# Two operand tiles of TensorE moved up by 32 bytes in SBUF

## The chip, the core and the metric

The kernel runs on one core of one Trainium2 chip. The metric is the time that the device takes for one execution, in microseconds (us). TensorE (PE) does the matrix products, VectorE (DVE) and ScalarE (ACT) the elementwise work, GpSimd (POOL) issues some transfers and SyncE (SP) the others. SBUF is the on-chip memory: 128 partitions, in each of which a tile lies at one byte address. A product on TensorE has a stationary operand, brought in by a weight load (LDWEIGHTS, "PEld" in the profile), and a moving operand, which the MATMUL instruction streams past it. Both are read from SBUF.

## The reference, cut to what matters

One decoder layer on 256 tokens of width 2048, in float32:

```
proj = x @ W_in                                    # q, k, v of 16 heads
mix  = concat(diff_attention, moba_attention) @ W_out
h    = LayerNorm(2**0.25 * x + mix)
u    = h @ W_up                                    # a gate and a value half, 5632 columns each
ffn  = (silu(causal_conv3(u_gate)) * u_value) @ W_down
out  = LayerNorm(2**0.25 * h + ffn)
```

## The kernel before, in words

**Number format.** TensorE works on float32r operands. To keep the accuracy of float32, each operand is split into a high part (ACT copies it to float32r, line 128 or 797) and a low part (DVE subtracts the high part, line 129 or 807; some low parts are made by an accumulating transfer, line 805). Each product is then three: high times high, high times low, low times high, all added up in PSUM.

**Operand tiles.** The input's parts are the tiles `xa` and `xb` (line 145), the normed tokens' parts `ha` and `hb` (line 528); both come from the helper `two` (line 139), under the tags `t2a` and `t2b` of the pool `keep`, so that h takes over the place of x. Each holds, for 8 chunks of 128 features, 256 high and 256 low values side by side, 16,384 bytes in a partition. Later three other tiles use the same places: `z2` (line 1356, tag `t2a`), `rawt` (line 1290) and `gb2` (line 1424, both `t2b`). Weights come through 4 buffers `raw` (1 MB each) into 6 buffers `hl` (high and low parts of 128x1024). Everything that TensorE reads as float32r begins, in every buffer, at a byte address that leaves 128 when it is divided by 512, and all slices of it that an instruction takes begin a multiple of 512 bytes further on. So any two float32r operands are at the same address modulo 512 bytes.

**Three kinds of products.** They differ in what moves and what stands still.

- *Pairs* (lines 206 to 211 for q and k, 831 to 834 for the up projection): a 128x128 block of the weights is stationary and the tokens move. The high block meets high and low tokens side by side, 512 columns; then the low block meets the high tokens alone, 256 columns. A pair of such instructions is done 16 times for each 128 features of the output:

```
for k in range(8 * x, 8 * x + 8):
    o = slice(k % 8 * P, k % 8 * P + P)
    mm(dst, wh[:, o], at_k(h2, k).rearrange("p j t -> p (j t)"), k == 0, False)
    mm(dst[:, 0:S], wl[:, o], at_k(h2, k)[:, 0], False, k == KT - 1)
```

- *Products with x or h stationary*: v (line 452, the weights move, 512 columns) and the first tile of the up projection (`mm_first`, lines 567 to 569, 256 columns).
- *All others*: the output projection (`mm_o`, line 499), the down projection (lines 1070 to 1072 and 1134 to 1136) and the last tiles (1365 to 1367). Their stationary operands are `mh`, `ml`, `aparts`, `pparts` and `tails`, the weights move, 512 columns mostly. They touch neither x nor h.

All of them go through the helper `mm`, so the profile names them all by line 202 and tells them apart by their tiles.

**Order of the work.** First v, q and k of four heads at a time, with the attention of earlier heads in between; then the output projection; the first LayerNorm with `mm_first`; then the up projection. From a certain tile on, products of the down projection come between its tiles, by a list that a planner in the kernel orders (lines 651 to 756, with costs and due times written in it). At the end come the last products of the down projection and the second LayerNorm. The planner knows nothing of addresses.

Of the kernel before, what the change touches and what calls it, by code (L numbers as in the profile page):

```python
# [11 lines left out]
F32 = mybir.dt.float32  # L12
# [4 lines left out]
P = 128  # L17
# [33 lines left out]
def hymba_layer(ctx: ExitStack, tc: tile.TileContext, a: dict):  # L51
# [3 lines left out]
    def pool(name, bufs=1, space=None):  # L55
        kw = {} if space is None else {"space": space}
        return ctx.enter_context(tc.tile_pool(name=name, bufs=bufs, **kw))

    keep = pool("keep")
    raws = pool("raws", 4)  # L60
    splits = pool("splits", 6)
    small = pool("small")
# [76 lines left out]
    def two(name):  # L139
        return [keep.tile([P, KT // 2, 2, S], F32R, name=f"{name}{j}", tag=f"t2{j}") for j in "ab"]  # L140
# [2 lines left out]
        return t[k // 8][:, k % 8] if n is None else t[k // 8][:, k % 8:k % 8 + n]  # L143

    x2 = two("x")
    z = keep.tile([P, 2, D], F32, name="z", tag="z")
    xraw = z.rearrange("p t d -> p (t d)")

# [1420 lines left out]
```

## Time and profile before

| | before |
|---|---|
| median of 3 runs | 1126.47 us (1125.85 to 1126.74) |
| the profiled execution's own time | 1125.76 us |
| its span, first to last instruction | 1124.0 us |
| PE busy | 1108.2 us, 99% |
| PE weight loads busy | 941.5 us, 84% |
| DVE busy | 917.3 us, 82% |
| ACT busy | 702.8 us, 63% |
| granted TensorE clock, mean | 0.996 |

Busy times of matmuls overlap: an instruction of 512 columns is in flight for some 390 ns, and the next one begins long before it ends. So the mean duration of a group is not the time that one of them takes of the engine; that is the distance from one start to the next, to be had from the number of instructions in a stretch in which PE never waits.

### The profile page before, as it was taken

What the parts mean: (1) busy time and instruction counts of PE and PEld (TensorE: products, weight loads), DVE (VectorE), ACT (ScalarE), POOL (GpSimd) and SP (SyncE); (2) the same over time, 40 slices, a digit from 0 to 9 for tenths busy, and PEclk for the clock granted to TensorE, in tenths of its full rate; (3) what the DMA queues carried; (4) which work ended last, traced back from release to release, by engine and by line L of the source; (5) the groups of instructions that cost most, each with busy time, mean ns of one, the idle gap of its engine ahead of it and who ended that gap; (6) DMA issues with size and microseconds to landing.
All of it is one profiled execution on the core that took longest, in us unless ns stands there. A gap on an engine that the chain in (4) does not pass through costs nothing.

```text
span 1124.0 us, 15532 instructions
## 1 busy us (share of the span) xinstructions
PE 1108.2 (99%) x5878; PEld 941.5 (84%) x5878; DVE 917.3 (82%) x1485; ACT 702.8 (63%) x1022; POOL 75.8 (7%) x90
## 2 busy tenths in 40 slices
PE   9999999999999999999999999999999999999995
PEld 6888888888888898888888888888888888888884
DVE  6886886867745787789999777798999888898997
ACT  6565465444544396767777666767767676767671
POOL 0000000000000000000100100000100010001104
PEclk9999999999999999999999999999999999999998
DMA  8755454545455637777897878777887698769883
GB/s 329 292 225 197 151 169 168 182 156 188 150 187 192 220 128 264 246 260 239 263 248 248 231 229 268 222 245 222 223 253 226 224 247 262 219 218 268 246 262 127
DMA packets 48507, 249.89 MB, mean 222 GB/s; under 512 B 4784, under 2 KB 6704, under 8 KB 27824
## 3 DMA queue, kind: packets, MB, share of 16 engines
q1 hardware_dynamic: 39360, 221.11, 55.0%
q0 software_dynamic: 9072, 27.79, 13.7%
q8 instruction: 46, 0.75, 0.3%
q14 instruction: 29, 0.24, 0.1%
HBM read 216.90 MB, written 9.44 MB: 201 GB/s over the span
## 4 chain that ended last, share of the span: by engine, by line
PE 93%; DVE 4%; DMA 1%; ACT 1%; issue 0%; POOL 0%; SPq 0%; POOLq 0%; ACTq 0%; DVEq 0%
PE bank L202 92%; DVE st L391 1%; DMA raw<-in_w_d 1%; DVE z L388 1%; PE bank L325 0%; DMA raw<-in_w_v 0%; DVE z L1460 0%; DVE bparts L1021 0%; DVE hl L1325 0%; DVE z L1371 0%; DVE spill L1384 0%; PE bank L542 0%; ACT bparts L1017 0%; DVE z L1456 0%; PE bank L372 0%
## 5 line engine op out<-in xcount | busy, mean ns | idle before, releaser
L202 PE MATMUL bank<-hb,hl 128*128 128x512 f32 x1376 | 256.7, 339 | 0.0
L202 PE MATMUL bank<-ha,hl 128*128 128x512 f32 x1376 | 255.6, 338 | 0.0
L202 PEld LDWEIGHTS bank<-ha,hl 128*128 128x128 f32 x1376 | 214.4, 188 | 33.7 <-ACT ev L901 0.4
L202 PEld LDWEIGHTS bank<-hb,hl 128*128 128x128 f32 x1376 | 210.7, 188 | 31.9
L129 DVE TENSOR_TENSOR hl<-raw,hl 128x1024 fp32r<-128x1024 f32 (+1 forms) x143 | 164.7, 1163 | 68.9 <-ACT hl L128 68.5
L128 ACT ACTIVATE hl<-raw 128x1024 fp32r<-128x1024 f32 (+1 forms) x143 | 143.7, 1009 | 92.8 <-PE bank L202 65.0
L807 DVE TENSOR_TENSOR hl<-raw,hl 128x1024 fp32r<-128x1024 f32 x128 | 154.9, 1221 | 20.9 <-ACT hl L797 20.4
L797 ACT ACTIVATE hl<-raw 128x1024 fp32r<-128x1024 f32 x128 | 133.0, 1052 | 35.1 <-PE bank L202 32.7
L901 ACT ACTIVATE ev<-bank 128x512 f32<-128x512 f32 x86 | 51.3, 597 | 96.5 <-PE bank L202 96.4
L202 PE MATMUL bank<-bparts,aparts 128*128 128x512 f32 x432 | 109.9, 392 | 0.8 <-DVE bparts L1021 0.8
L1021 DVE TENSOR_TENSOR bparts<-sums,bparts 128x1024 fp32r<-128x1024 f32 x72 | 85.9, 1222 | 20.0 <-ACT bparts L1017 20.0
L202 PE MATMUL bank<-xa,hl 128*128 128x512 f32 (+1 forms) x512 | 97.7, 344 | 0.0
L202 PE MATMUL bank<-xb,hl 128*128 128x512 f32 (+1 forms) x512 | 96.3, 341 | 0.0
L202 PEld LDWEIGHTS bank<-bparts,aparts 128*128 128x128 f32 x432 | 78.4, 188 | 18.2 <-DVE bparts L1021 1.6
L202 PEld LDWEIGHTS bank<-xa,hl 128*128 128x128 f32 x512 | 78.9, 188 | 13.5 <-issue 1.3
L202 PEld LDWEIGHTS bank<-xb,hl 128*128 128x128 f32 x512 | 78.4, 189 | 11.7
L1017 ACT ACTIVATE bparts<-sums 128x1024 fp32r<-128x1024 f32 x72 | 73.2, 1054 | 17.4 <-PE bank L202 8.1
L805 POOL DMA_DIRECT2D hl<-raw x39 | 34.1, 875 | 548.2 <-ACT hl L795 377.7
L202 PE MATMUL bank<-hl,mh 128*128 128x512 f32 x256 | 70.4, 392 | 0.0
L202 PE MATMUL bank<-hl,aparts 128*128 128x512 f32 x252 | 65.4, 391 | 0.0
L795 ACT ACTIVATE hl<-raw 128x1024 fp32r<-128x1024 f32 x39 | 41.2, 1055 | 29.8 <-PE bank L202 29.7
L202 PEld LDWEIGHTS bank<-hl,mh 128*128 128x128 f32 x256 | 47.7, 188 | 9.7
(167 smaller groups left out, 1426.7 us busy)
## 6 DMA issues: line engine op xcount, KB each, us to landing
raw<-in_w_u SPq DMA_DIRECT2D x88, 1024.0 KB, 5.6
raw<-in_w_d SPq DMA_DIRECT2D x42, 1024.0 KB, 6.7
raw<-in_w_qk SPq DMA_DIRECT2D x32, 1024.0 KB, 4.8
hl<-raw POOLq DMA_DIRECT2D x41, 512.0 KB, 5.4
raw<-in_w_o SPq DMA_DIRECT2D x16, 1024.0 KB, 4.8
raw<-in_w_v SPq DMA_DIRECT2D x12, 1024.0 KB, 4.8
zd<-spill POOLq DMA_DIRECT2D x20, 256.0 KB, 7.5
raw<-in_w_v SPq DMA_DIRECT2D x8, 256.0 KB, 4.6
```

Source lines behind the costliest of these rows:

```text
L128: ACT.activation(hi[:, s], t[:, x:y], AF.Copy)
L129: DVE.tensor_tensor(lo[:, s], t[:, x:y], hi[:, s].bitcast(F32), ALU.subtract)
L202: PE.matmul(out, lhsT, rhs, start=start, stop=stop)
L388: DVE.scalar_tensor_tensor(z[:, t, s], z[:, t, s], alpha, src, op0=ALU.mult, op1=ALU.add)
L391: DVE.bn_stats(stats[ln, t][:, c], z[:, t, s])
L795: ACT.activation(lo, raw_of[n][:, s], AF.Copy, scale=-1.0)
L797: ACT.activation(hi, raw_of[n][:, s], AF.Copy)
L805: POOL.dma_start(lo, raw_of[n][:, s], accum_op=ALU.add)
L807: DVE.tensor_tensor(lo, raw_of[n][:, s], hi.bitcast(F32), ALU.subtract)
L901: ACT.activation(evs[n], bank[b], AF.Copy)
L1017: ACT.activation(U()["b", j][:, 0], U()["T"][:, 2 * j:2 * j + 2], AF.Copy)
L1021: DVE.tensor_tensor(b[:, 1], U()["T"][:, 2 * j:2 * j + 2], b[:, 0].bitcast(F32), ALU.subtract)
```

## The change

Two tiles are added to the pool `keep`. One of 32 bytes lies ahead of `xa` and `xb`, one of 480 bytes behind them. Nothing reads or writes them. By that, `xa`, `xb`, `ha`, `hb`, and the later tiles on their places (`z2`, `rawt`, `gb2`), begin at an address that leaves 160 when it is divided by 512, 32 bytes more than before. All tiles behind them lie 512 bytes higher, so their address modulo 512 is the same as before, 128 for all other float32r operands.

```diff
@@ -57,6 +57,7 @@
     keep = pool("keep")
+    shift = keep.tile([P, 8], F32, name="shift")
     raws = pool("raws", 4)
     splits = pool("splits", 6)
@@ -143,6 +144,7 @@
     x2 = two("x")
+    back = keep.tile([P, P - 8], F32, name="back")
     z = keep.tile([P, 2, D], F32, name="z", tag="z")
```

The instructions, their order on each engine, their waits and the transfers are the same, one by one; only addresses differ.

## The prediction

> **What bounds the kernel now.** I read the page first: the share of each engine, the clock row and the summary of the chain that ended last.
>
> ```profile
> span 1124.0 us, 15532 instructions
> PE 1108.2 (99%) x5878; PEld 941.5 (84%) x5878; DVE 917.3 (82%) x1485; ACT 702.8 (63%) x1022; POOL 75.8 (7%) x90
> PEclk9999999999999999999999999999999999999998
> PE 93%; DVE 4%; DMA 1%; ACT 1%; issue 0%; POOL 0%; SPq 0%; POOLq 0%; ACTq 0%; DVEq 0%
> ```
>
> TensorE is never short of work, its clock is granted in full, and 93% of the last chain is its own matmuls. So the time is set by how far apart the matmuls start. The only thing that this change can touch is that distance, and it touches it only if it depends on where the operands lie. Next I looked in the chain of waits, told in order of time, for long pieces of PE without a wait; the columns are start, length, engine and count.
>
> ```profile
> 413.37 69.35 PE bank L202 x400
> 485.60 578.32 PE bank L202 x3061
> ```
>
> The first piece is the up projection alone: 400 matmuls are 200 pairs (one of 512 columns, one of 256), so a pair takes 69.35 / 200 = 346.8 ns. The second piece is the up projection with products of the down projection between its tiles. Its content is in the groups by line and shape for 486 to 1063 us, with a count, the busy time and the mean ns of one instruction:
>
> ```profile
> L202 PE MATMUL bank<-hb,hl 128*128 128x512 f32 x584 | 210.0, 399 | 0.0
> L202 PE MATMUL bank<-ha,hl 128*128 128x512 f32 x584 | 208.7, 397 | 0.0
> L202 PE MATMUL bank<-hb,hl 128*128 128x256 f32 x584 | 164.0, 281 | 0.0
> L202 PE MATMUL bank<-ha,hl 128*128 128x256 f32 x584 | 163.8, 281 | 0.0
> L202 PE MATMUL bank<-bparts,aparts 128*128 128x512 f32 x416 | 105.6, 391 | 0.6 <-DVE bparts L1021 0.6
> L202 PE MATMUL bank<-hl,aparts 128*128 128x512 f32 x204 | 53.7, 391 | 0.0
> L202 PE MATMUL bank<-one,aparts 128*128 128x512 f32 x102 | 28.9, 391 | 0.0
> ```
>
> That is 1168 pairs and 416 + 204 + 102 = 722 products of 512 columns. What such a product takes is seen in the output projection, where nothing else runs. The two rows are a stretch in the table of windows (length, PE busy, count) and the group in it, with its mean of 389 ns:
>
> ```profile
> 326.00:370.00 44.00, 44.00 (x196) 36.44 (x195) 23.00 (x22) 17.41 (x17) 0.00 (x0) 1.00 0.57 191
> L202 PE MATMUL bank<-hl,mh 128*128 128x512 f32 x131 | 35.1, 389 | 0.0
> ```
>
> The count includes the one in flight at the edge, so the distance is (44.00 + 0.39) / 196 = 226.5 ns. The 722 products then take 163.5 us of the 577 us, and the pairs (577 - 163.5) / 1168 = 354.0 ns each. **The same pair of instructions, on the same tiles at the same addresses, takes 346.8 ns in one stage and 354.0 ns in the other.** PE waits for nobody in either. The groups of the pure stage (414 to 482 us) show where the 7.2 ns are: the instructions themselves are longer, 399/397 against 393/394 ns and 281 against 277 ns.
>
> ```profile
> L202 PE MATMUL bank<-hb,hl 128*128 128x512 f32 x101 | 35.6, 393 | 0.0
> L202 PE MATMUL bank<-ha,hl 128*128 128x512 f32 x96 | 33.8, 394 | 0.0
> L202 PE MATMUL bank<-hb,hl 128*128 128x256 f32 x101 | 28.0, 277 | 0.0
> L202 PE MATMUL bank<-ha,hl 128*128 128x256 f32 x96 | 26.6, 277 | 0.0
> ```
>
> And the q and k projections, in a stretch without anything else (29 to 45 us), have the durations of the slower state:
>
> ```profile
> L202 PE MATMUL bank<-xa,hl 128*128 128x512 f32 x24 | 8.6, 398 | 0.0
> L202 PE MATMUL bank<-xa,hl 128*128 128x256 f32 x24 | 6.7, 281 | 0.0
> ```
>
> So a pair has at least two steady states, and what it enters depends on how the run of pairs begins. That is how two readers of one memory behave that get in each other's way: the moving stream and the weight load run at the same time, from addresses that are equal modulo 512 bytes, and their relation settles into a pattern. I take this as the theory; the trace doesn't prove that the relation goes by address and not by time alone.
>
> **The change part by part.** No instruction is added, removed or moved, on any queue, and no wait is added. Four things get other addresses.
>
> *Pairs* (the moving operand 32 bytes higher, the stationary one where it was). Their number in the whole trace:
>
> ```profile
> L202 PE MATMUL bank<-hb,hl 128*128 128x512 f32 x688 | 246.7, 398 | 0.0
> L202 PE MATMUL bank<-ha,hl 128*128 128x512 f32 x688 | 245.4, 397 | 0.0
> L202 PE MATMUL bank<-xa,hl 128*128 128x512 f32 x256 | 93.8, 406 | 0.0
> L202 PE MATMUL bank<-xb,hl 128*128 128x512 f32 x256 | 92.5, 401 | 0.0
> ```
>
> 688 + 688 + 256 + 256 = 1888 pairs, 200 of them in the better state, 1688 in the worse. An operand at another offset has no row in this trace, so the cost is bounded from both sides. Below: a 512 at 226.5 ns and a 256 at half of that make 339.8 ns, 14.2 less than now, 1688 x 14.2 + 200 x 7.0 = 25.4 us saved. Above: one more step of 7.2 ns, and the pure stage thrown back as well, 1688 x 7.2 + 200 x 14.4 = 15.0 us lost. Between them I take the row that exists: the shift changes the relation from which every run of pairs starts, most pairs are now in the worse of the two states seen, and there are more ways to leave it downward than upward. All 1888 pairs at 346.8 ns: 1688 x 7.2 = 12.2 us saved.
>
> The Trainium skill, "TensorE: Matmul & The Clock Gate", in the step-by-step part of what happens when a matmul is issued, says that TensorE has two independent read ports, so that loading the next weights takes no bandwidth from the running matmul. By that rule no address could matter and the sum would be zero. The trace doesn't bear out its independence as far as duration goes: the same instruction has means of 393 and 399 ns, with no wait in either.
>
> *Products with x or h stationary*: 192 + 192 for v, and 48 + 48 of 256 columns in `mm_first`.
>
> ```profile
> L202 PE MATMUL bank<-hl,xa 128*128 128x512 f32 x192 | 47.5, 399 | 0.5 <-DVE hl L129 0.2 <-ACT hl L128 0.2
> L202 PE MATMUL bank<-hl,xb 128*128 128x512 f32 x192 | 46.4, 395 | 0.0
> L202 PE MATMUL bank<-hl,ha 128*128 128x256 f32 x48 | 6.8, 291 | 0.7 <-DVE ha L557 0.7
> L202 PE MATMUL bank<-both,hb 128*128 128x256 f32 x48 | 6.4, 286 | 0.0
> L202 PE MATMUL bank<-hl,xb 128*128 128x512 f32 x42 | 9.7, 389 | 0.0
> ```
>
> The last row is a stretch of v without waits (19.2 to 28.4 us): 389 ns, the same as in the output projection, so v is already at the best that a 512 shows. It can hardly gain; if it loses a step of 7.2 ns each, that is 384 x 7.2 = 2.8 us. I take half, 1.4 us lost. The 96 of `mm_first` are too few to matter: a step is 0.7 us either way, taken at nothing.
>
> *Writers and transfers.* ACT and DVE write the four tiles, and transfers fill `rawt`, `z2` and `gb2` on their places at the end.
>
> ```profile
> L155 ACT ACTIVATE xa<-z x8: 400/402/418, 2.9 to 12.9; 128x256 fp32r<-128x256 f32 x8
> L557 DVE TENSOR_TENSOR ha<-hf,ha x4: 680/692/693, 395.1 to 404.2; 128x512 fp32r<-128x512 f32 x4
> z<-zd SPq DMA_DIRECT2D x1, 2048.0 KB, 8.2
> rawt<-in_w_d SPq DMA_DIRECT2D x2, 1024.0 KB, 10.0
> ```
>
> The spread of the writes (400 to 418 ns, 4%) on the few that stand on the path between the output and the up projection, some 5 us, is 0.2 us. A tenth more for the transfers would be 1 us each; at the end, DVE's own work covers them for the most part, and without that cover the 1 us is lost. I take both at nothing and keep 1.2 us for the range.
>
> *What is late next* where pairs get faster: DVE, which splits the weights. In the busiest long stretch it has this share (the third busy time):
>
> ```profile
> 700.00:930.00 230.00, 230.00 (x1214) 196.28 (x1213) 205.50 (x285) 163.05 (x203) 19.14 (x22) 1.00 0.77 234
> ```
>
> 205.5 of 230 is 89%. The forecast shortens a stretch by 2%, which makes it 91%; the lower bound makes it 93%. So DVE gives no new wait of any length.
>
> *Sum*: -12.2 + 1.4 = -10.8 us. Against the profiled execution's own time, 1125.76 us (its span of 1124.0 and 1.8 around it), this gives 1115.0; that execution lies 0.7 us below the median of the three runs, 1126.47, so for the median I write 1115.7 us.
>
> **The rivals.**
>
> *A better pattern than any pair shows now.* The relation gets free of the collision, and a pair takes 339.8 ns or a little less: -25.4 + 1.4 = -24.0 us, 1102.5 us. For it: v and the output projection hold 226.5 ns over hundreds of instructions. Against it: the shift is small, and no pair in the trace gets there. Chance 0.12.
>
> *Nothing happens.* The states come from the times at which the two reads begin, not from addresses: then the same instructions in the same order settle as before, 1126.5 us. For it: the two states arise at the same addresses. Against it: nothing but the start of a run tells the stages apart, which address and time share. Chance 0.18. This is also what the rule of the skill quoted above would give.
>
> *Slower: the moving stream's lead grows.* The moving operand starts just ahead of its weight load; 32 bytes more push it further ahead, and the two meet earlier in every load and for longer. The place is every pair; it decides as soon as a pair takes over 354.0 ns on average. Price: 15.0 us as worked out above, and 1.4 for v: 1142.9 us. If only the pure stage is thrown into the worse state and v loses its step, it is 1.4 + 2.8 = 4.2 us. For it: the products in which all operands are at one address are the ones that run best, 226.5 ns, so equal addresses may be the good case. Against it: the pairs have equal addresses too, and 1688 of 1888 are in the worse state seen. Chance 0.34.
>
> **How the numbers follow.** The forecast itself, pairs at about 346.8 ns, has 0.36, the deeper gain 0.12, no change 0.18, slower 0.34. A measurement of this kernel can tell about 0.2%, some 2.3 us, from no change. Faster by more: 0.36 + 0.12 = 0.48. Within: 0.18. Slower: 0.34. The range goes from 1101 us, the deeper gain with the writers' 1.2 us in its favour, to 1142 us, which covers the slower case but for its end. Left out are a collision that goes away altogether or one that is several steps worse. Since cases of both signs hold most of the chance, the forecast's own range is 1112 to 1120 us.
>
> **What would show it.** In the profile after, the groups of pairs between 486 us and the end should have means of about 394 and 277 ns, and the long piece of the chain should be some 8 us shorter for the same count. The output projection is the control, with no operand moved: 226.5 ns apart, 389 ns long, as before. V should show at most 7 ns more. The forecast is wrong if the pairs' means stay at 398 and 281 (address doesn't matter), if they rise, or if the pairs get shorter and PE begins to wait for DVE's low parts instead.

## The result and the profile after

The changed kernel takes 1118.70 us (median of 6 runs, 1117.88 to 1119.91), the kernel before beside it 1126.61 us (6 runs, 1125.45 to 1128.07): a ratio of 0.9931, with an interval from 0.9918 to 0.9944. It is 7.9 us faster; 10.8 were forecast. The profiled execution took 1117.88 us, with a span of 1116.1.

The page of the changed kernel: span, busy time by engine, and the summary of the chain that ended last.

```profile
span 1116.1 us, 15532 instructions
PE 1100.2 (99%) x5878; PEld 944.9 (85%) x5878; DVE 916.6 (82%) x1485; ACT 702.3 (63%) x1022; POOL 75.9 (7%) x90
PE 93%; DVE 4%; DMA 1%; ACT 1%; issue 0%; SPq 0%; POOL 0%; POOLq 0%; ACTq 0%; DVEq 0%
```

The count of instructions is the same, and PE lost 8.0 us of busy time where the span lost 7.9. DVE, ACT and POOL kept their shares, and the weight loads have 85% where they had 84%, so it is the matmuls that stand closer together. Where, the chain of waits tells (start, length, engine, count; line 202 of before is line 204 now). Of before, these three pieces are quoted that the prediction did not show; the two others stand there.

```profile
105.02 26.49 PE bank L202 x152
181.22 26.10 PE bank L202 x148
319.85 72.80 PE bank L202 x322
```

And the same pieces of the changed kernel, with the two of the up projection:

```profile
105.22 26.02 PE bank L204 x152
181.16 25.63 PE bank L204 x148
318.57 72.80 PE bank L204 x322
411.95 69.35 PE bank L204 x400
484.18 571.85 PE bank L204 x3061
```

The first two, in the attention stage, are each 0.47 us shorter. The third holds the output projection, with no moved operand for most of it, and is the same to the hundredth. So is the up projection alone (x400). The last piece, up and down projection interleaved, went from 578.32 to 571.85 us: 6.5 us of the 7.9.

The timeline shows it tile by tile. Each row of 16 is eight pairs of one half of the features; columns are start and length. First the kernel before, in the middle of the last piece:

```profile
703.35 2.97 PE L202 MATMUL bank<-ha,hl 128*128 128x512 f32 x16
706.16 2.99 PE L202 MATMUL bank<-hb,hl 128*128 128x512 f32 x16
708.99 1.55 PE L202 MATMUL bank<-bparts,aparts 128*128 128x512 f32 x6
710.38 1.52 PE L202 MATMUL bank<-hl,aparts 128*128 128x512 f32 x6
711.74 2.97 PE L202 MATMUL bank<-ha,hl 128*128 128x512 f32 x16
```

Then the changed one:

```profile
704.87 1.54 PE L204 MATMUL bank<-bparts,aparts 128*128 128x512 f32 x6
706.24 1.52 PE L204 MATMUL bank<-hl,aparts 128*128 128x512 f32 x6
707.60 2.96 PE L204 MATMUL bank<-ha,hl 128*128 128x512 f32 x16
710.39 2.94 PE L204 MATMUL bank<-hb,hl 128*128 128x512 f32 x16
713.16 0.86 PE L204 MATMUL bank<-one,aparts 128*128 128x512 f32 x3
```

From start to start, 16 pairs took 708.99 - 703.35 = 5.64 us before, 352.5 ns each, and take 713.16 - 707.60 = 5.56 us now, 347.5 ns each. The 12 products between took 711.74 - 708.99 = 2.75 us, 229.2 ns each, and now 2.73, 227.5 ns, though nothing of theirs was moved. Look at what the mean durations do meanwhile (whole trace, by shape; they answer to the rows of 688 and 192 in the prediction). The first line, of 256 columns, is of the kernel before, the others are of the changed one:

```profile
L202 PE MATMUL bank<-hb,hl 128*128 128x256 f32 x688 | 192.8, 280 | 0.0
L204 PE MATMUL bank<-ha,hl 128*128 128x512 f32 x688 | 243.5, 392 | 0.0
L204 PE MATMUL bank<-hb,hl 128*128 128x512 f32 x688 | 242.3, 390 | 0.0
L204 PE MATMUL bank<-hb,hl 128*128 128x256 f32 x688 | 194.2, 282 | 0.0
L204 PE MATMUL bank<-hl,xa 128*128 128x512 f32 x192 | 48.1, 404 | 0.5 <-ACT hl L129 0.5
L204 PE MATMUL bank<-hl,xb 128*128 128x512 f32 x192 | 47.5, 400 | 0.2 <-DVE hl L130 0.2
```

The 512s of a pair fell from 397/398 to 392/390 ns, while the 256s rose from 280 to 282: a pair's gain isn't the sum of what its durations lost. V rose by 5 ns.

For the whole program I added up, over the records of the trace, the distance from each matmul's start to the next one's, by the kind of the first; a long distance, in which PE waited, counts as the usual one of its kind. So the sums are good to some 0.4 us, their differences between kernels to some 0.2. This table (in us) is used for all kernels below:

| | v, 384 | q and k, 512 pairs | output projection, 384 | up, 1376 pairs | down projection |
|---|---|---|---|---|---|
| before | 87.7 | 180.6 | 87.3 | 483.9 | 215.3 |
| changed | 89.5 | 177.6 | 87.2 | 478.2 | 214.5 |

The differences are +1.8, -3.0, -0.1, -5.7 and -0.8, together -7.8 us of the 7.9. In the single starts there is a pattern: before, three pairs of the interleaved stage repeat as 236/113, 233/117 and 241/120 ns (512 to 256, 256 to the next), 1060 ns or 353.3 a pair; in the pure stage two repeat as 231/112 and 233/117, 346.7 a pair. Now the first three pairs of a run take 355, 353 and 352 ns, and then all are 228/118, 346.7.

### The profile page after: what moved, and what is told of

Its sections match the earlier page's. It is cut to its first block, busy times and chain, and to the rows that moved or that the text cites. A ratio compares the mean times of both kernels' runs of the same rounds, so it can differ in the third digit from the quotient of the medians.

```text
span 1116.1 us, 15532 instructions
## 1 busy us (share of the span) xinstructions
PE 1100.2 (99%) x5878; PEld 944.9 (85%) x5878; DVE 916.6 (82%) x1485; ACT 702.3 (63%) x1022; POOL 75.9 (7%) x90
## 4 chain that ended last, share of the span: by engine, by line
PE 93%; DVE 4%; DMA 1%; ACT 1%; issue 0%; SPq 0%; POOL 0%; POOLq 0%; ACTq 0%; DVEq 0%
PE bank L204 93%; DMA raw<-in_w_v 1%; DVE st L393 1%; DVE z L390 1%; PE bank L327 0%; DVE z L1462 0%; DVE z L1373 0%; DVE hl L1327 0%; DVE spill L1386 0%; DVE bparts L1023 0%; PE bank L544 0%; SPq L152 0%; ACT bparts L1019 0%; DVE z L1458 0%; PE bank L374 0%
## 5 line engine op out<-in xcount | busy, mean ns | idle before, releaser
L204 PE MATMUL bank<-hb,hl 128*128 128x512 f32 x1376 | 252.7, 336 | 0.0
L903 ACT ACTIVATE ev<-bank 128x512 f32<-128x512 f32 x86 | 51.3, 597 | 89.5 <-PE bank L204 89.5
```

The source lines that it names most:

```text
L204: PE.matmul(out, lhsT, rhs, start=start, stop=stop)
L903: ACT.activation(evs[n], bank[b], AF.Copy)
```

## The experiments

Two theories stood against each other at first. **A**: the relation of the moving operand's address to the weights' decides, as the prediction has it; its direction (further ahead or behind) then sets the sign. **B**: the moving operand's own address decides, and that of the weights doesn't matter. Times are medians; each kernel before ran on the same chip beside it (1126.40 to 1126.50 us).

**Everything 32 bytes higher.** Against the changed kernel, the second added tile goes, so that all float32r operands lie 32 bytes higher and are at one address modulo 512 again:

```diff
-    back = keep.tile([P, P - 8], F32, name="back")
```

Expected:

> Every tile 32 bytes higher (the small tile ahead of x stays, the one behind it goes), so all float32r operands are at one address modulo 512 again, but another one. Theory A, the difference between moving and stationary address counts: as the kernel before, v and output projection 226.5 ns apart, the run of pairs between the products 354 ns a pair, 1126.6 us within 2.3. Theory B, the moving operand's own address counts: pairs as in the changed kernel, 346.7 ns, and the products whose moving operand is a weight tile change too, so the output projection leaves 226.5 ns; not over 1121 us if they gain, over 1130 if they lose 7 ns each as v did.

Measured: 1126.19 us, ratio 0.9999 (0.9989 to 1.0008). The chain has the pieces of before, to the hundredth:

```profile
413.17 69.35 PE bank L203 x400
485.40 578.32 PE bank L203 x3061
```

and the table's row is the row of before (87.7, 180.6, 87.3, 483.9, 215.3). B falls: x and h lie where the changed kernel has them, and nothing is gained. What counts is whether the weights lie at the same place. Order and waits are the same in all three kernels, and only the one with another relation differs; so timing alone, the rival "nothing happens", falls too.

**32 bytes lower.** The same distance the other way:

```diff
-    shift = keep.tile([P, 8], F32, name="shift")
+    shift = keep.tile([P, P - 8], F32, name="shift")
...
-    back = keep.tile([P, P - 8], F32, name="back")
+    back = keep.tile([P, 8], F32, name="back")
```

Expected:

> The tiles of x and h 480 bytes higher, which is 32 bytes lower modulo 512; the two small tiles swap places, nothing else. Theory A: the pairs have the relation that v had in the changed kernel (moving 32 bytes below stationary), and v has the one that the pairs had there. If the sign counts, the pairs lose, over 354 ns each, 1127 to 1145 us, and v is back near 226.5 ns. Theory B with a period of 64 bytes: as the changed kernel, 1118.7 us, since 32 and 480 are the same modulo 64.

Measured: 1122.46 us, ratio 0.9969 (0.9958 to 0.9981), between the two kernels. The profiled execution is among the longer ones, 1124.09 us of 1120.26 to 1124.21. Its piece of the up projection alone:

```profile
415.15 70.67 PE bank L204 x400
```

The pure stage is thrown into the worse state, 70.67 / 200 = 353.4 ns a pair (240/120 and 230/117 in turn), while the interleaved pairs settle at 346.6 ns. The table: v 89.3, q and k 179.9, up 479.0, down 215.8, with 1.0 us more of waiting in v and 0.9 in the up projection. The mirror image of a gain is not a loss: A's direction falls, and with it the picture of a moving stream that runs further ahead of the load. The relation matters, but each value has a distance of its own, and here one relation has two of them, 353.4 ns in the pure stage and 346.6 between products.

**A map of relations.** So I measured them by themselves, in one run. This kernel leaves out the layer (its output is a copy of x). One stationary tile `wa`, and moving tiles `ma` to `mp` that begin 0, 32, 64 ... 480 bytes higher modulo 512; for each, 32 pairs, later 24 products of 512 and 24 of 256 columns, with 12 products of 512 at one common address between the runs:

```
for o in t:
    pairs(w[0], t[o], 32)
    chain(last, last, 12, 512)
```

Expected:

> Not the layer: runs of matmuls alone on tiles written once, the output is a copy of x. 32 pairs, 24 of 512 columns and 24 of 256 columns, with the moving tile 0, 32, ... 480 bytes above the stationary one; two half steps (16 and 48); pairs with both tiles 32 and both 256 higher; pairs at 0 and at 32 after transposes instead of after a chain. Theory A: both 32 higher gives the same as both at 0 (353 to 354 ns), moving 32 higher gives 346.7, moving 480 higher with 512 columns gives the 233 ns of v in the changed kernel. Theory B: both 32 higher gives 346.7. After transposes the pairs at 0 fall into 346.8 ns as in the pure stage before, those at 32 stay at 346.7.

While the pairs run, TensorE has the memory nearly for itself. In the table of windows the columns behind PE and its weight loads are DVE, ACT and POOL, then the granted clock, the transfers' share and GB/s:

```profile
34.00:300.00 266.00, 266.00 (x1453) 230.26 (x1453) 0.00 (x0) 0.00 (x0) 0.00 (x0) 1.00 0.00 1
```

So what this map shows needs no other engine. The timeline of PE, with start and length of each run; the distance is the next run's start less this one's, over 32 pairs or 24 products:

```profile
34.26 11.45 PE L74 MATMUL bank<-ma,wa 128*128 128x512 f32 x64
45.55 2.94 PE L74 MATMUL bank<-last 128*128 128x512 f32 x12
48.34 11.28 PE L74 MATMUL bank<-mb,wa 128*128 128x512 f32 x64
59.45 2.90 PE L74 MATMUL bank<-last 128*128 128x512 f32 x12
...
145.74 11.45 PE L74 MATMUL bank<-mi,wa 128*128 128x512 f32 x64
157.03 2.95 PE L74 MATMUL bank<-last 128*128 128x512 f32 x12
...
312.83 5.60 PE L74 MATMUL bank<-ma,wa 128*128 128x512 f32 x24
318.27 2.88 PE L74 MATMUL bank<-last 128*128 128x512 f32 x12
320.99 5.77 PE L74 MATMUL bank<-mb,wa 128*128 128x512 f32 x24
326.59 2.92 PE L74 MATMUL bank<-last 128*128 128x512 f32 x12
```

At the same address (`ma`) 32 pairs take 45.55 - 34.26 = 11.29 us, 352.8 ns a pair with the run's start in it; 32 bytes higher 59.45 - 48.34 = 11.11 us, 347.2 ns; 256 bytes higher (`mi`) 11.29 us again. The products of 512 columns go the other way: 5.44 / 24 = 226.7 ns at the same address, 5.60 / 24 = 233.3 ns at 32 bytes. Those are the sizes of the two effects of the change, without the layer around them. (In v the weights move, 32 bytes lower than x, so its column is that of 224 bytes, with 233.2 ns.) All settled distances in ns, read from the single starts, are means over the last 24 pairs or 12 products of a run:

| bytes higher | 0 | 32 | 64 | 96 | 128 | 160 | 192 | 224 |
|---|---|---|---|---|---|---|---|---|
| pair | 353.3 | 346.7 | 348.9 | 350.0 | 351.1 | 346.7 | 353.3 | 346.7 |
| 512 columns | 226.7 | 233.3 | 229.0 | 233.4 | 233.3 | 234.6 | 233.4 | 233.2 |
| 256 columns | 120.0 | 116.7 | 117.9 | 120.0 | 120.1 | 118.9 | 117.9 | 118.1 |

From 256 to 480 bytes the eight values of each row come again. So the relation repeats after 256 bytes, not 512, and 32 bytes lower is the column of 224. Moving both operands by 256 leaves a pair at 353.3; moving both by 32 gave 346.7, the better of the two states of relation 0 (231/113 and 232/117), which the layer shows in its pure stage. Behind four transposes, as the pure stage begins, I had expected that better state for relation 0; it stayed at 353.3. What chooses between the two is open.

**Only h moved.** The slots are 32 bytes longer, x begins at their start and h 32 bytes higher (against the changed kernel, whose `shift` and `back` go). Here, and with 16 and 28 bytes below, `xb` and `hb` come to lie another 256 bytes further on modulo 512, which by the map is the same relation:

```diff
+        o = {"x": 0, "h": 8}[name]
...
+            t = keep.tile([P, KT * S + 8], F32R, name=f"{name}{j}", tag=f"t2{j}")
+            out.append(t[:, o:o + KT * S].rearrange("p (k j t) -> p k j t", j=2, t=S))
+            if name == "x":
+                keep.tile([P, 56], F32, name=f"back{j}")
```

Expected:

> Only h lies 32 bytes higher than the other float32r operands modulo 256 bytes; x lies where all the others do (the places of x and h are 32 bytes longer, and h begins 32 bytes into them). Theory A with the period of 256 bytes that the map showed: v goes back to 226.7 ns and saves the 1.8 us that it lost in the changed kernel, q and k go back to 353 ns a pair and lose the 3.0 us that they had gained, the up projection stays at 346.7: 1119.9 us, 1.2 above the changed kernel. If the gain of the changed kernel came from the places of x at the start or of the late tiles, the up projection shows nothing of it and the time is over 1122.

Measured: 1120.44 us, ratio 0.9944 (0.9927 to 0.9961). The pieces of the attention stage are those of before, the long piece is that of the changed kernel:

```profile
106.14 26.49 PE bank L209 x152
182.34 26.10 PE bank L209 x148
414.39 69.36 PE bank L209 x400
486.63 571.85 PE bank L209 x3061
```

So the parts are separate: h brings the larger part, and x the rest, gain in q and k and loss in v together. The table agrees: v 87.6 and q and k 180.7 as before, up 478.2 and down 214.5 as changed.

**16 bytes.** The same code with `{"x": 4, "h": 4}`, to see whether steps of 32 bytes are what counts.

> x and h both 16 bytes higher modulo 256. Theory A: pairs settle at 346.7 ns, as the map has for 16 bytes; v has the relation of -16 bytes, which the map didn't have, between 226.7 and 235 ns. 1116 to 1120 us, and below the changed kernel only if v stays under 231 ns. Rival: only whole steps of 32 bytes count, so 16 bytes is as 0: 1126.5 us.

Measured: 1120.35 us, ratio 0.9942 (0.9927 to 0.9957). Pairs gain as they do with 32 bytes (q and k 178.0, up 478.5), v loses less (88.4), but the products of the down projection take 216.5, 2.0 more than in the changed kernel. That is a little worse than forecast, by the products behind the pairs. The first map has this too: the 12 products behind the pairs at 16 bytes (from 268.33 to 271.10 us) took 230.8 ns each, those behind the pairs at 32 bytes (from 59.45 to 62.19 us) 228.3. A step of half of 32 bytes acts, so 32 is no unit of it.

**192 bytes.** The map has a relation in which pairs stay at 353.3 ns: nothing gained. V, in which the weights move, has the opposite one, the column of 64 bytes, with 229.0 ns against 226.7: a little lost. `shift` is 48 floats and `back` P - 48.

> x and h 192 bytes higher. Theory A by the map: pairs settle at 353.5 ns, in the pure stage as well, which loses 1.3 us there; v has the relation of -192, the same as 64: 229.0 ns, 0.9 us lost; 1127 to 1129 us. Rival, that any other address than the common one helps: about 1119 us.

Measured: 1129.23 us, ratio 1.0024 (1.0014 to 1.0033): slower than before, as the map says, and 0.2 us over the forecast's end. Two pieces:

```profile
415.14 70.67 PE bank L204 x400
488.68 579.20 PE bank L204 x3061
```

The pure stage goes to 353.4 ns a pair, 1.3 us longer, and the interleaved piece is 0.9 us longer than before.

**Finer maps.** Two more kernels in the manner of the first map (the layer left out), each run once, took offsets between its points.

> The map again, not the layer (the output is a copy of x): the moving tile 16, 48, ... 240 bytes above the stationary one, and 4, 8, 24, 28, 36 and 40 bytes. Theory A: each relation has a distance of its own, pairs from 346 to 354 ns, and no relation gets below 340 ns a pair or 226 ns for 512 columns, since the weight load of 128 columns meets the moving stream at some point whatever the start. Rival: only steps of 32 bytes count, and what lies between two steps has the value of the lower one (353.5 for 4 to 28 bytes, 346.7 for 36 to 48).

> The map again (no layer, the output is a copy of x): pairs and 512 columns with the moving tile 12, 28, 44, ... 252 bytes above the stationary one, and 512 columns with it 4, 20, ... 244 above, which are the relations that v gets where x is one of the first lot higher. Theory A: 28 gives 343.3 ns again, and a pair somewhere among 12, 28, 44, 60 comes to 340 to 346 ns; nothing gets below 340 a pair. If the 343.3 was a matter of what ran before it, 28 gives another value now, since other runs stand ahead of it.

Settled distances in ns, from the two maps (28 bytes is in both, with the same 343.3 behind other runs; 236 bytes, in the second, has 343.3 too):

| bytes higher | 4 | 8 | 12 | 16 | 24 | 28 | 36 | 40 | 44 | 48 | 60 | 80 | 240 |
|---|---|---|---|---|---|---|---|---|---|---|---|---|---|
| pair | 360.0 | 353.3 | 346.7 | 346.7 | 360.0 | 343.3 | 360.0 | 353.3 | 346.7 | 346.7 | 343.3 | 353.3 | 353.3 |

Two runs of the first of them, which carry the ends of that range (`mi` is 4 bytes, `ml` 28):

```profile
139.98 11.68 PE L74 MATMUL bank<-mi,wa 128*128 128x512 f32 x64
151.50 2.95 PE L74 MATMUL bank<-last 128*128 128x512 f32 x12
...
182.59 11.15 PE L74 MATMUL bank<-ml,wa 128*128 128x512 f32 x64
193.58 2.92 PE L74 MATMUL bank<-last 128*128 128x512 f32 x12
```

(151.50 - 139.98) / 32 = 360.0 ns and (193.58 - 182.59) / 32 = 343.4 ns: 4.6% between two places of the same data. 512-column products are at 226.7 ns at the same address only; elsewhere they are between 228.3 and 240.0. No pair came below 343.3. The rival of whole steps falls, since 28 bytes has not the value of 0, nor 36 that of 32; and the pairs spread wider than the 346 to 354 ns that I had expected of them.

**28 bytes.** The best pair of the map, put into the layer: the same code with `{"x": 7, "h": 7}`.

> x and h both 28 bytes higher modulo 256, the relation that gave the shortest pair in the second map. Theory A: up projection and q, k settle near 343.3 ns a pair, 3.4 ns less than in the changed kernel, 1888 x 3.4 = 6.4 us less at most; v has the relation of -28 bytes, which no run has shown: the relations 4 bytes past a step of 16 had 235 to 237 ns, so up to 1.4 us more than in the changed kernel. 1112 to 1118 us. If what counts in the layer is how a run of pairs begins and not what it settles at, no better than the changed kernel, 1118.7.

Measured: 1113.28 us (1112.47 to 1113.49), ratio 0.9882 (0.9869 to 0.9896). It beats both kernels, the changed one by 5.3 us on the same chip (1118.56, below). The pure stage, and two tiles of the interleaved one on the timeline:

```profile
410.15 68.68 PE bank L209 x400
```

```profile
701.50 1.55 PE L209 MATMUL bank<-bparts,aparts 128*128 128x512 f32 x6
702.89 1.53 PE L209 MATMUL bank<-hl,aparts 128*128 128x512 f32 x6
704.27 2.91 PE L209 MATMUL bank<-ha,hl 128*128 128x512 f32 x16
707.01 2.91 PE L209 MATMUL bank<-hb,hl 128*128 128x512 f32 x16
709.76 0.86 PE L209 MATMUL bank<-one,aparts 128*128 128x512 f32 x3
```

A pair takes 68.68 / 200 = 343.4 ns alone and (709.76 - 704.27) / 16 = 343.1 ns between products: the run of pairs has no slower head. The 12 products lose a little of it, 2.77 / 12 = 230.8 ns. The table: v 89.6, q and k 175.8, up 472.4, down 216.1.

**The changed kernel again**, on the chip of the last ones:

> The changed kernel as it is, beside the one with 28 bytes, for a comparison on the same chip: 1118.7 us within 2.

Measured: 1118.56 us, ratio 0.9932 (0.9919 to 0.9946), and a table row equal to the first.

## Why the prediction was right, and where it was off

*What bounds the kernel.* Right: PE is at 99%, 93% of the last chain is its matmuls, and the whole change of the span is the sum of their distances.

*Two states of a pair.* Right in kind. The distance of 354.0 ns was too long by 1.5: the sum took the products between the pairs at 226.5 ns, as in the output projection, but the first few after each run of pairs take longer (231 to 236 ns, and 229.2 in the mean of the 12 above). I put their loss down to the pairs, which are at 352.5. That the start of a run decides which state it enters was not borne out: in the map, pairs at equal addresses settle at 353.3 ns behind products and behind transposes alike.

*Pairs, -12.2 us.* The step that was mis-sized: measured 3.0 + 5.7 = 8.7 us. Of the 3.5 missing, 1.5 ns x 1176 interleaved pairs = 1.8 us never was theirs; the three slower pairs at the head of each run hold the mean at 347.7 instead of 346.8, 0.9 x 1176 = 1.1 us; the rest, 0.7, is q and k, where I had 7.2 ns a pair and 5.9 came ((180.6 - 177.6) / 512). The distance that pairs settle at, 346.7 ns, is the forecast one, but by another pattern than the row from which I took it (228/118 against 231/112 and 233/117). Nothing in that row told what 32 bytes would give, and by the maps other offsets give 343.3 to 360.0: that the size came out is in part luck.

*V, 1.4 us lost.* 1.8 measured, within the bounds of 0 and 2.8, of which I had taken half without a reason. V is now at 89.5 / 384 = 233.1 ns, as the map has it for 224 bytes; before it was at 87.7 / 384 = 228.4, not quite at the best.

*Taken at nothing.* `mm_first` went from 13.0 to 12.9 us. The output projection has the same distance, with the length, busy time and count of PE at the head of the row: (44.00 + 0.39) / 196 = 226.5 ns.

```profile
325.00:369.00 44.00, 44.00 (x196) 36.45 (x195) 23.29 (x22) 17.50 (x17) 0.00 (x0) 1.00 0.56 193
```

What I had not on the list is the 0.8 us of the down projection: its operands stayed, but it starts behind pairs in another state. Writers and transfers cost nothing that shows: behind the long piece the span goes on for 60.1 us in both kernels.

*DVE as the next wait.* No new wait: gaps in which PE waited in the up projection add up to 0.2 us in both. The share came to

```profile
694.00:924.00 230.00, 230.00 (x1227) 199.15 (x1226) 207.71 (x288) 163.38 (x204) 19.15 (x22) 1.00 0.77 237
```

207.71 of 230, 90%, against 91% forecast.

*What would show it.* The long piece lost 6.5 us, not 8. The means of 394 and 277 ns did not come (391 and 282): that a duration tells the state was wrong, since the good state exists with 394/277 and with 391/282. Distances do tell it.

*The rivals.* "Nothing happens" falls by the changed kernel beside the one with everything 32 bytes higher. It also was what the Trainium skill's rule of two independent read ports would give ("TensorE: Matmul & The Clock Gate", on the steps of a matmul). This case does not bear that out: the same 24 products took 226.7 or 233.3 ns by the relation of the two addresses alone. The deeper gain was not reached with 32 bytes, but 28 bytes goes half the way to its 339.8 ns. The slower case exists too, at 192 bytes, at 2.8 us rather than 16; its mechanism, a growing lead, fell with the changed kernel, in which 32 bytes more gained, and with the run 32 bytes lower. So the sign rested on an argument that was no mechanism ("more ways to leave it downward"), and the runs bear it out for this offset: of the eight relations in steps of 32, none is above the one that the kernel had. It does not hold for every small offset: 24 and 36 bytes have 360.0 ns in the finer maps. That the sign came out is in part luck as well.

*Open.* What in the memory repeats after 256 bytes; what chooses between the two states of equal addresses, and of 32 bytes lower (353.4 ns in the layer's pure stage, 346.7 in the map); and why 4, 24 and 36 bytes are the worst and 28, 60 and 236 the best. That the two reads collide in SBUF is the reading that fits, and in the maps nobody else was at work; but it is not shown: only their addresses were changed, nothing was seen of the port.

## What to carry to other kernels

Where TensorE is the bound and waits for nobody, take the distance from start to start of each kind of product, in a stretch without anything else and in a mixed one; if the same instruction has two distances, the relation of its two operands' addresses is worth a map. Such a map costs one small kernel, and its best pair, 343.3 ns, came out the same in the layer (472.4 / 1376 = 343.3). Not every value of it does, as 32 bytes lower tells, so the layer has the last word. Read the state from distances, never from mean durations, and charge what lies between two kinds of products to neither.

## What the runs showed of the hardware

- With float32r operands and a weight load for each product, the distance depends on the difference of the moving and the stationary address: 343.3 to 360.0 ns for a pair of 512 and 256 columns, 226.7 to 240.0 ns for 512 columns, 113.3 to 123.3 for 256. In steps of 32 bytes it repeats after 256 bytes.
- Single steps of 4 bytes matter: 24 bytes is at 360.0, 28 at 343.3, 32 at 346.7 ns.
- A pair is not the sum of its parts: at the same address 226.7 + 120.0 = 346.7 ns against the 353.3 that it takes there, and 32 bytes apart 233.3 + 116.7 = 350.0 against 346.7.
- A product takes over something of the state before it: with its own operands unmoved, the 12 products behind the pairs take 229.2, 227.5 or 230.8 ns by where the pairs' operands lie.
